# A tiled 90-degree rotation: fewer TensorE outputs in the first macro tile and the last but one, and a different split of the copies

## The chip, the core and the metric

The kernel runs on one core of one Trainium2 chip. The metric is the device time of one execution in microseconds; the median of three runs is given. The engines are TensorE (PE, with its weight loads as PEld), VectorE (DVE), ScalarE (ACT), GpSimd (POOL) and SyncE (SP). Sixteen DMA engines move the data between HBM and the on-chip memory.

## The reference

```python
x = np.random.randn(8192, 8192).astype(np.float32)   # k = 1
return np.rot90(x, k)
```

The output is the input turned by 90 degrees: row i of the output is column 8191 - i of the input. Nothing is computed. 268.4 MB are read, 268.4 MB are written, and on the way each block must be transposed with its columns in reversed order.

## The kernel before, in words

**Tiles.** The input is cut into 16 macro tiles (`kk` 0 to 15) of 1024 rows by 4096 columns. A macro tile has T = 8 loads of 128 rows x 4096 columns (2 MB each; load m belongs to macro tile m // 8 and is called row tile t = m % 8) and J = 8 outputs (n = 8 kk + j; 512 input columns by 1024 rows, 2 MB each).

**Buffers.** Five buffers of 2 MB: buffers 0 and 1 take the landings, 2 to 4 the finished outputs. In the first macro tile loads 0 to 4 use all five, then load 5 goes to buffer 0, 6 to 1, 7 to 2, 8 to 4, 9 to 0, 10 to 1, 11 to 0 and so on by turns. Outputs 0 to 7 use buffers 3, 2, 4, 3, 2, 4, 3, 2. Between them stands `ring`, 63 slots of 128 x 512 elements; a row tile fills eight slots, and the slots that output t of one macro tile leaves free take row tile t of the next.

**Two ways of turning a block.** `by_pe(kk)` lists the outputs that are turned by TensorE. For these DVE copies the landed columns to the ring with the order reversed (`tensor_copy`), TensorE transposes 32 blocks of 128 x 128 into PSUM, and ACT copies PSUM into the output buffer (three copies). For all other outputs ("moved" outputs) DVE transposes within squares of 32 x 32 as it copies to the ring (`transpose`, STREAM_TRANSPOSE in the profile), and 16 copies of 32 x 1024 elements (`moves`) then put the squares in place. `shares(n)` gives the first `BY_DVE` = 3 of these moves to DVE, the next `BY_POOL` = 8 to POOL, and the remaining 5 to ACT. In the last macro tile the split is 6, 6 and 4.

Before the change TensorE turns all eight outputs of macro tile 0, outputs 0 and 4 of macro tiles 1 to 13, outputs 0, 2, 4, 6, 7 of macro tile 14 (the last but one) and 0, 1, 3, 5, 7 of macro tile 15.

**Order on the engines.** Each engine runs its own list in order.

- SP issues loads 1, 3, 5 and half of loads 6 to 9, and then all stores in the order of n. It waits for POOL's last move of a moved output (`s_pool`), or for ACT's last copy of the others.
- ACT issues the other loads. Load n + 9 stands behind output n in ACT's list: `load_behind(n)` puts it in front of the first copy of an output of TensorE, behind all of ACT's moves of a moved output, or behind the third one if the output before was TensorE's. A load waits until the row tile before it in its buffer has been copied out (`taken`).
- POOL makes its share of the moves; its last one waits for the shares of ACT and DVE (`s_act`, `s_dve`).
- DVE takes row tile m = n + 8 after its moves of output n, and only once output n has left the ring: it waits for `s_pool` of a moved output, or for TensorE (`s_half`).
- The 512 columns of the last output in the last row tile of each macro tile have no slot: DVE copies them within the landing buffer, and TensorE turns them there (the "corner") before it turns the last row tile of output 0. In that row tile DVE takes the columns in the order of `got`: output 0's, the moved ones, the corner, the remaining ones of TensorE.

Copies with equal operands in successive pairs of macro tiles run as a loop (`Program.play` with `first` and `times`): ACT and POOL loop over macro tiles 1 to 12, DVE and TensorE over 2 to 13; the others are written out.

```python
        (nc.gpsimd, by_gpsimd, 1, 6),
        (nc.vector, by_vector, 2, 6),
        (nc.tensor, by_tensor, 2, 6),
        (nc.scalar, by_scalar, 1, 6),
```

All recorded instructions stand under line 106 (`Op.run`) in the profile.

Of the kernel before, what the change touches and what calls it, by code (L numbers as in the profile page):

```python
# [13 lines left out]
J = W // (G * P)  # L14
# [6 lines left out]

Q = 32
BY_DVE = 3
BY_POOL = 8
LAST_DVE = 6
LAST_POOL = 6
LAST_PE = [0, 1, 3, 5, 7]
BY_PE = [0, 4]
# [147 lines left out]
def kernel(tc: tile.TileContext, x: bass.AP, k: bass.AP, out: bass.AP):  # L176
    nc = tc.nc
# [6 lines left out]
    KK = len(macros)  # L184
# [11 lines left out]
    outs = [(*o, [(j, g * P) for j in reversed(o[2]) for g in range(G)]) for o in outs]  # L196

    def by_pe(kk):
        if kk == 0:
            return list(range(J))  # L200
        if kk == KK - 1:
            return LAST_PE
        return BY_PE if kk < KK - 2 else [*range(0, J, 2), J - 1]

    def in_quadrants(kk, j):
        return j not in by_pe(kk)
# [127 lines left out]
    for m in range(n_load):  # L334
        kk, t = divmod(m, T)
        here = by_pe(kk)
        rest = [j for j in range(J) if j not in here]
        if kk == KK - 1:
            got = [here, rest] if t < T - 1 else [here[:1], here[1:-1], rest, here[-1:]]
        elif t < T - 1:  # L340
            got = [here, rest]
        else:
            inner = [j for j in here if 0 < j < J - 1]
            got = [here[:1], [j for j in rest if j < J - 1], [J - 1], inner]
        got = [part for js in got for part in split(js)]
        pieces[m] = got
        for js in got:
            done += 1
            for j in js:
                rev[m, j] = done  # L350
# [37 lines left out]
    def shares(n):  # L388
        d, g = (BY_DVE, BY_POOL) if n < n_out - J else (LAST_DVE, LAST_POOL)
        return pairs[:d], pairs[d : d + g], pairs[d + g :]  # L390
# [243 lines left out]
    for e, by, first, times in (  # L634
        (nc.sync, by_sync, None, 0),
        (nc.gpsimd, by_gpsimd, 1, 6),
        (nc.vector, by_vector, 2, 6),
        (nc.tensor, by_tensor, 2, 6),
        (nc.scalar, by_scalar, 1, 6),
    ):  # L640
        program = Program()
        by(program)
        program.play(nc, e, first, times)
# [39 lines left out]
```

## Time and profile before

| | |
|---|---|
| median of 3 runs | 1258.81 us (1258.65 to 1258.83) |
| the profiled execution | 1258.87 us; its span 1257.5 us |
| busy: DVE, POOL, ACT, PE | 783.5, 749.2, 601.7, 293.6 us |
| DMA | 537.05 MB, mean 427 GB/s over the span |
| moves: POOL, ACT, DVE | 666, 417, 261 instructions |
| TensorE transposes | 1460 |

The span runs from the first to the last recorded instruction; the time of the execution has 1.4 us around it. The rows of slices give busy tenths in 40 equal parts of the span, and the row of GB/s gives what the DMA engines moved in each. A group of instructions is read as: line, engine, operation, output <- input, number; then total busy time and the mean of one. In a timeline the first two numbers are the start and the length in microseconds.

### The profile page before, as it was taken

The page shows a single profiled execution, that of the slowest core. Times are in us where ns is not written, and L with a number is a line of the kernel's source. Part 1 is how long each engine was busy: PE and PEld are TensorE (multiplying, and loading weights), DVE is VectorE, ACT ScalarE, POOL GpSimd, SP SyncE. Part 2 cuts the span into 40 slices and gives each one's busy share as a digit, 9 for nine tenths or more (in the row PEclk, how much of TensorE's full clock was granted, in tenths as well). Part 3 has the DMA queues.
Part 4 walks back from the last instruction along what each step waited for, and adds up shares of the span by engine and source line. Part 5 has one row for each costly group of instructions (what it writes and reads, how often), then busy time and mean ns, then how long its engine had stood idle before and what let it go on. Part 6 is the DMA issues. An engine that isn't in the chain of part 4 may idle for free.

```text
span 1257.5 us, 6240 instructions
## 1 busy us (share of the span) xinstructions
PE 293.6 (23%) x1460; PEld 257.4 (20%) x1460; DVE 783.5 (62%) x568; ACT 601.7 (48%) x562; POOL 749.2 (60%) x672
## 2 busy tenths in 40 slices
PE   1566013130131301213022130221302213024261
PEld 0455012120121201212012120221302213023261
DVE  2544866567666676566765667656666566664563
ACT  0334364553655436544365443654436544364374
POOL 0000966668656686666866668666685666864334
PEclk9977556555565655655555555555555555556587
DMA  9999999999999999999999999999999999999999
GB/s 400 416 432 427 430 429 429 429 430 429 431 428 430 430 429 430 429 430 430 430 429 429 429 430 429 430 429 430 429 429 429 429 430 429 430 427 430 428 419 384
DMA packets 36942, 537.05 MB, mean 427 GB/s; under 512 B 4160, under 2 KB 4160, under 8 KB 4160
## 3 DMA queue, kind: packets, MB, share of 16 engines
q1 hardware_dynamic: 19184, 278.93, 52.2%
q10 hardware_dynamic: 17744, 257.96, 48.0%
q8 instruction: 6, 0.10, 0.0%
q14 instruction: 8, 0.07, 0.0%
HBM read 268.44 MB, written 268.44 MB: 427 GB/s over the span
## 4 chain that ended last, share of the span: by engine, by line
DMA 70%; DVE 20%; POOL 3%; issue 3%; PE 1%; ACTq 0%; ACT 0%; DVEq 0%; POOLq 0%; SPq 0%
DMA buf<-in_x_dram 69%; DVE ring L106 18%; POOL buf L106 3%; DVE buf L106 2%; DMA out_dram<-buf 1%; PE ps L106 1%; ACTq L106 0%; ACT buf L106 0%; DVEq L103 0%; DVEq L147 0%; ACTq L103 0%; POOLq L153 0%; POOLq L103 0%; ACTq L430 0%; SPq L422 0%
## 5 line engine op out<-in xcount | busy, mean ns | idle before, releaser
L106 POOL COPY buf<-ring 32x1024 f32<-32x1024 f32 (+1 forms) x666 | 748.5, 1124 | 488.1 <-DMA out_dram<-buf 216.2
L106 ACT COPY buf<-ring 32x1024 f32<-32x1024 f32 (+1 forms) x417 | 427.3, 1025 | 190.1 <-DMA out_dram<-buf 140.0
L106 PE MATMUL ps<-head,ring 128*128 128x128 f32 x1400 | 280.5, 380 | 878.4 <-ACT buf L106 550.1
L106 PEld LDWEIGHTS ps<-head,ring 128*128 128x128 f32 x1400 | 247.2, 202 | 908.9 <-ACT buf L106 560.2
L106 DVE COPY ring<-buf 128x1024 f32<-128x1024 f32 (+4 forms) x159 | 149.0, 947 | 452.6 <-DMA buf<-in_x_dram 415.0
L106 ACT COPY buf<-ps 128x2048 f32<-128x2048 f32 (+4 forms) x143 | 173.2, 1253 | 444.4 <-DMA out_dram<-buf 179.6
L106 DVE STREAM_TRANSPOSE ring<-buf 128x3072 f32<-128x3072 f32 (+1 forms) x133 | 372.1, 2805 | 0.0
L106 DVE COPY buf<-ring 32x1024 f32<-32x1024 f32 (+1 forms) x261 | 274.6, 1052 | 2.5
L106 PE MATMUL ps<-head,buf 128*128 128x128 f32 x60 | 16.1, 422 | 63.1 <-DVE buf L106 63.1
L106 PEld LDWEIGHTS ps<-head,buf 128*128 128x128 f32 x60 | 10.5, 211 | 68.6 <-issue 61.2
L106 DVE COPY buf<-buf 128x512 f32<-128x512 f32 x15 | 5.8, 387 | 0.0
L106 ACT ACT_TABLE_LOAD x1 | 1.3, 1283 | 3.3 <-PEq L430 3.3
L106 POOL MEMSET head<- 128x128 f32 x1 | 0.2, 204 | 2.8 <-POOLq L430 2.8
L106 POOL TENSOR_SCALAR_AFFINE_SELECT head<-head 128x128 f32<-128x128 f32 x1 | 0.3, 292 | 0.2 <-POOL head L106 0.2
L664 POOL MEMSET const-float32-0.0<- 128x1 f32 x1 | 0.1, 97 | 0.2 <-issue 0.2
L106 ACT COPY head<-head 128x1 f32<-128x1 f32 x1 | 0.2, 191 | 0.0
L664 POOL MEMSET const-bfloat16-1.0<- 128x1 bf16 x1 | 0.1, 100 | 0.0
L664 POOL MEMSET const-uint8-127<- 128x1 uint8 x1 | 0.1, 100 | 0.0
L664 POOL MEMSET const-float32-1.0<- 128x1 f32 x1 | 0.1, 98 | 0.0
## 6 DMA issues: line engine op xcount, KB each, us to landing
out_dram<-buf SPq DMA_DIRECT2D x128, 2048.0 KB, 16.7
buf<-in_x_dram ACTq DMA_DIRECT2D x121, 2048.0 KB, 15.2
buf<-in_x_dram SPq DMA_DIRECT2D x3, 2048.0 KB, 17.3
buf<-in_x_dram SPq DMA_DIRECT2D x4, 1024.0 KB, 16.0
buf<-in_x_dram ACTq DMA_DIRECT2D x4, 1024.0 KB, 16.6
```

The source lines that it names most:

```text
L106: i = getattr(e, self.name)(*self.args, **kwargs)
L664: nc = _bacc.Bacc("TRN2", target_bir_lowering=False, num_devices=1)
```

## The change

Three things are changed. TensorE turns only outputs 0 and 4 of macro tile 0, as in the macro tiles after it, and outputs 0, 4, 6, 7 of macro tile 14. For moved outputs outside the last macro tile POOL makes seven moves and ACT six. And TensorE's loop covers macro tiles 1 to 12, so that macro tile 13 is written out and macro tile 1 is in the loop.

```diff
-BY_POOL = 8
+BY_POOL = 7
...
     def by_pe(kk):
-        if kk == 0:
-            return list(range(J))
         if kk == KK - 1:
             return LAST_PE
-        return BY_PE if kk < KK - 2 else [*range(0, J, 2), J - 1]
+        return BY_PE if kk < KK - 2 else [*BY_PE, J - 2, J - 1]
...
-        (nc.tensor, by_tensor, 2, 6),
+        (nc.tensor, by_tensor, 1, 6),
```

With `BY_PE = [0, 4]` seven outputs go from TensorE to moves: 1, 2, 3, 5, 6 and 7 of macro tile 0, and 2 of macro tile 14.

## The prediction

> **What bounds the kernel now.** I read the page first, above all its rows of slices.
>
> ```profile
> DMA  9999999999999999999999999999999999999999
> GB/s 400 416 432 427 430 429 429 429 430 429 431 428 430 430 429 430 429 430 430 430 429 429 429 430 429 430 429 430 429 429 429 429 430 429 430 427 430 428 419 384
> ...
> q8 instruction: 6, 0.10, 0.0%
> ...
> DMA 70%; DVE 20%; POOL 3%; issue 3%; PE 1%; ACTq 0%; ACT 0%; DVEq 0%; POOLq 0%; SPq 0%
> ```
>
> The DMA engines are busy in every slice and move the same 429 or 430 GB/s in all but the first two and the last two. No compute engine is above 62%. So an edit can change the time only where it changes what the DMA engines lose, and they lose little. The trace's packet records say how little: a packet of 16 KB takes 0.611 us, a load or store of 2 MB is 128 packets on 16 engines, so 8 x 0.611 = 4.89 us, and 256 of them are 1251.3 us. The first packet starts at 1.96. 1253.3 is thus the floor of a span of 1257.5.
>
> The windows of the span, in steps of 20 us and then of 2, show where the other 4.2 us are (columns: stretch, length, busy of PE, PEld, DVE, ACT, POOL with counts, clock, DMA share, GB/s).
>
> ```profile
> 40.00:60.00 20.00, 13.19 (x76) 11.67 (x76) 10.53 (x8) 8.28 (x7) 0.00 (x0) 1.00 1.00 410
> ...
> 600.00:620.00 20.00, 0.00 (x0) 0.00 (x0) 14.55 (x10) 9.77 (x10) 17.96 (x16) 0.50 1.00 428
> ...
> 1222.00:1224.00 2.00, 1.73 (x8) 1.73 (x9) 1.98 (x2) 2.00 (x3) 1.84 (x2) 0.51 0.87 369
> 1224.00:1226.00 2.00, 2.00 (x14) 2.00 (x13) 1.97 (x3) 1.98 (x3) 1.96 (x2) 0.64 0.82 344
> ...
> 1254.00:1256.00 2.00, 0.00 (x0) 0.00 (x0) 0.00 (x0) 0.00 (x0) 0.00 (x0) 0.50 0.10 41
> ```
>
> In packets: 0.44 us go to slow packets in the first 5 us and 0.82 between 49 and 53, where loads 0 to 9 end and store 0 begins (packets of 1.1 us, share still 1.00). Store 122 comes late at 1223.6 and costs 15 engines about 0.5. At the end 15 engines stop by 1254.6 and one goes on alone to 1257.1: it is 2.5 us behind. In the middle nothing is lost, though DVE, ACT and POOL work as they will after the change.
>
> Then the timeline of the head, which is what the change rebuilds.
>
> ```profile
> 13.23 4.49 DVE L106 COPY ring<-buf 128x4096 f32<-128x4096 f32 x2 [13.23 <-DMA buf<-in_x_dram]
> ...
> 37.76 2.29 DVE L106 COPY ring<-buf 128x4096 f32<-128x4096 f32 x1 [0.58 <-DMA buf<-in_x_dram]
> ...
> 42.56 0.43 DVE L106 COPY ring<-buf 128x512 f32<-128x512 f32 x1 [2.51 <-DMA buf<-in_x_dram]
> ...
> 43.50 0.71 PEld L106 LDWEIGHTS ps<-head,buf 128*128 128x128 f32 x4 [2.68 <-DVE buf L106]
> ...
> 46.12 74.13 SPq L106 DMA_DIRECT2D out_dram<-buf  x9
> ...
> 63.78 0.69 DVE L106 COPY ring<-buf 128x1024 f32<-128x1024 f32 x1 [6.65 <-DMA buf<-in_x_dram]
> 64.39 3.37 DVE L106 STREAM_TRANSPOSE ring<-buf 128x3072 f32<-128x3072 f32 x1
> ...
> 112.59 0.43 DVE L106 COPY ring<-buf 128x512 f32<-128x512 f32 x1 [5.73 <-DMA buf<-in_x_dram]
> 112.93 2.90 DVE L106 STREAM_TRANSPOSE ring<-buf 128x1536 f32<-128x1536 f32 x2
> 115.75 0.39 DVE L106 COPY buf<-buf 128x512 f32<-128x512 f32 x1
> ...
> 122.55 4.21 ACT L106 COPY buf<-ring 32x1024 f32<-32x1024 f32 x4 [2.87 <-DMA out_dram<-buf]
> ```
>
> DVE now needs 2.3 us for a row tile of macro tile 0 and waits for each landing; a mixed tile, as at 63.78, takes 3.98. Store 0 is issued at 46.12, while the queues still hold loads 8 and 9, and load 10 at 45.5 (ACT's queue). So the DMA never runs dry.
>
> **Part 1: macro tile 0, the DVE.** Row tiles 0 to 6 cost 3.98 instead of 2.3. Loads land in pairs at 13.23, 23.00, 32.68, then at 37.76 and 42.56. Tiles 0 and 1: 13.23 to 21.19. Tiles 2, 3: 23.00 to 30.96. Tiles 4, 5: 32.68 to 36.66 and 40.64. Tile 6 (landed 37.76): 40.64 to 44.62. So far this hides: the landings still come as before, because load 8 is issued at 36.7 and load 9 at 40.6, and the DMA reaches them only at 1.96 + 0.44 + 8 x 4.89 = 41.5 and at 46.4. Loads 0 to 9 end at 51.3.
>
> Tile 7 starts at 44.62 instead of 42.56. Its corner copy now stands behind the moved columns: 115.75 - 112.59 = 3.16 later, 47.78, done at 48.17, TensorE at 48.21. From TensorE's corner to store 0 the trace has 46.12 - 43.50 = 2.62, so store 0 goes out at 50.83, 4.7 us later than now.
>
> **Part 2: load 10.** This is the step that costs. Before, output 1 is TensorE's and load 10 is issued in front of its first copy. After, output 1 is a moved one, and for j = 1 `load_behind` puts the load behind all of ACT's moves, so load 10 stands behind six of them. ACT is free at 50.8; six at 4.21 / 4 = 1.05 are 6.3, so load 10 is issued at 57.2.
>
> What hides that wait is store 0 alone. From issue to first packet on idle engines I take 1.2 us: store 122 is issued at 1223.61 in the timeline and its packets start at 1224.82 (the first load, at the very start, took 1.04). Store 0 runs from 52.0 to 56.9; then the engines wait until 57.2 + 1.2 = 58.4. Store 1 can't help: DVE's three moves stand behind tile 8 (50.2 to 54.2, it waits for TensorE's output 0) and end at 57.4, POOL's last move ends at 58.5.
>
> By 58.4 eleven transfers are done: 58.4 - 1.96 - 11 x 4.89 = 2.7 us lost, where the kernel now has lost 0.44 + 0.82 = 1.26. **Net 1.4 us later.** Whether the slow packets around 50 return does not matter, since they fall into the gap. Slow packets at the restart: none to 0.44, the amount of the start; I take 0.2.
>
> Trainium skill, "DMA: Bandwidth & Descriptors", section "Latency and other measured facts", gives about 0.6 us to the first byte for these queues; by that the net would be 0.8 instead of 1.4 (estimate). The trace has 1.04 and 1.2 and I go by it.
>
> From there the queues fill: load 10 and store 1 give work to 68.2, load 11 is issued behind output 2's moves at 63.7 and store 2 at 67, load 12 at 71. Each is early by 3 us or more. DVE's new wait for POOL's output 1 at tile 9 (to 58.5) delays that tile and load 11 behind it, within this margin.
>
> **Part 3: seven moves for POOL, six for ACT.** Each moved output costs POOL 1.12 less and ACT 1.05 more. Between macro tiles 2 and 13 loads that stand behind all of an output's moves are issued at least 2.0 us after ACT's last move (ACT's rows against its issues), because they wait for DVE; so 1.05 more is hidden, and nothing is lost there anyway (600 to 620). Without that cover it would be 1.05 per load only once both queues were empty. Gain: none, as POOL is not the bound. Zero, with -0.2 to +0.3 for ends.
>
> **Part 4: output 2 of macro tile 14 and TensorE's loop.** The macro tile then has the pattern of tiles 1 to 13, which runs at 429 GB/s, with two TensorE outputs at its end. POOL gets 7 x 1.12 = 7.9 us within an output's 9.8. Zero; the late store 122 may move by its own 0.5 either way, but the engine that ends last is behind by more than that gap and does not see it.
>
> **Part 5: instructions fetched.** TensorE loses 6 x 32 - 4 + 32 = 220 transposes, so 440 instructions with the weight loads. The six 16 KB packets of q8 are TensorE's: between those at 58.2 and 97.2 it runs 256 recorded instructions. 440 are 1.7 packets of 0.6 to 1.0 us less. Each delays one DMA engine, and only the last one counts: 0 to -1.7, I take one packet, -0.6. The instructions that DVE, ACT and POOL gain are fetched in 8 KB packets of 0.31: +0.3 at most, the same doubt.
>
> **Sum.** 1.4 + 0.2 - 0.6 = +1.0 on 1258.87, 1259.9; the median lies 0.06 below its profiled execution, so 1259.8. A measurement can tell about 0.2% from no change, 2.5 us here; this is within.
>
> **The rivals.**
>
> *A, slower: POOL and DVE take turns.* If DVE's copies kept POOL from moving, each moved output would cost POOL 7.9 + 3.2 + 0.7 = 11.8 instead of 7.9, more than the 9.8 that a load and a store need. Outputs 1 to 3 and 5 to 7 would then each be 2 us late, with empty queues in the head: first at store 2, then at 3, some 3 us in all after the queues' reserve. It decides from 9.8 per output. 1259.8 + 3 = 1262.8. For: POOL's moves go from 1.03 to 1.40 beside DVE's. Against: macro tiles 1 to 13 run eight such moves with no loss. 0.12. Trainium skill, "SBUF — State Buffer", section "Who interferes with whom", has such a lock between GpSimd and DVE copies; POOL's mean of 1124 ns over 666 moves does not bear out a full block.
>
> *B, no difference: the fetches pay for the gap.* 1.4 - 1.7 = -0.3 and quick restart: 1258.5. For: the last engine's lag has steps of 0.6 at 58 and at 616, after instruction packets. Against: the packet at 97 hit another engine. 0.25.
>
> *C, the lagging engine catches up.* It works on while others wait, so gaps shrink its 2.5 us. If all of it goes: 1258.8 + 1.6 - 2.5 = 1257.9, and with all of part 5 besides 1256.2. Its lag is still under 1 us in the head, so the new gaps come too early. 0.08, of which a quarter for the lower value.
>
> **How the numbers follow.** Forecast 0.55 (1259 to 1261.2), A 0.12, B 0.25, C 0.08. Slower by over 0.2%, above 1261.3: most of A and a little of the forecast, if load 10 is 1.5 us later than summed, 0.13. Faster: 0.02. Range: B's and C's upper part to the lower edge of A, 1257.9 to 1261.8.
>
> **What would show it.** Right: GB/s of 40 to 60 at about 380 instead of 410 (20 us less 2.2 to 2.5, at 429); store 0 issued near 50.8, load 10 near 57.2; no loss from 70 to 1220; 1240 transposes on PE; POOL 634 moves, some 713 us, ACT 540 moves; fewer q8 packets. Wrong: a second dip between 60 and 90 (A), load 10 before 56, or all engines ending together (C).

## The result, and the profile after

The changed kernel takes 1260.37 us (median of 20 runs, 1260.01 to 1260.84) against 1258.78 us (20 runs, 1258.57 to 1259.09): 1.6 us more, a ratio of 1.0013, 95% interval 1.0007 to 1.0018. It is a small loss that these runs can tell from none, and within the 0.2% that the prediction counted as no change.

The page of the changed kernel, rows of slices, the queue of TensorE's instructions and the chain:

```profile
DMA  9999999999999999999999999999999999999999
GB/s 399 402 432 427 430 430 429 431 427 431 429 431 429 429 431 428 431 429 431 429 429 431 428 431 429 431 429 429 431 428 431 429 430 430 429 431 427 432 417 385
...
q8 instruction: 4, 0.07, 0.0%
...
DMA 71%; DVE 20%; issue 4%; POOL 2%; ACT 1%; PE 0%; ACTq 0%; DVEq 0%; POOLq 0%; SPq 0%
```

The middle is what it was. The second slice falls from 416 to 402, and the last two hardly move. POOL has 634 moves and 694 us, ACT 540 moves and 702 us, TensorE 1240 transposes: the work went where the diff sends it.

Windows of the changed kernel (stretch, length, busy of PE, PEld, DVE, ACT, POOL, clock, DMA share, GB/s):

```profile
40.00:60.00 20.00, 6.45 (x27) 5.35 (x27) 16.91 (x14) 13.35 (x13) 9.34 (x9) 0.92 0.99 406
600.00:620.00 20.00, 0.00 (x0) 0.00 (x0) 13.53 (x11) 11.88 (x12) 15.19 (x14) 0.50 1.00 428
...
50.00:52.00 2.00, 1.65 (x8) 1.65 (x9) 2.00 (x2) 1.96 (x3) 1.92 (x3) 1.00 0.83 352
54.00:57.00 3.00, 0.00 (x0) 0.00 (x0) 2.97 (x3) 2.95 (x4) 2.07 (x2) 0.99 1.07 344
60.00:63.00 3.00, 0.00 (x0) 0.00 (x0) 3.00 (x2) 2.94 (x3) 2.92 (x3) 0.50 0.96 300
```

Three places lose. Around 51 the share falls to 0.83: the engines are idle for 0.34 us. At 54 to 57 and at 60 to 63 the share is about 1.00, yet little is moved: the packets are slow. In the packet records each of the 16 engines has a packet of 1.20 us instead of 0.61 at 55.4 to 55.8, right before load 10's first packet at 56.6, and packets of up to 1.25 us before store 1's first at 62.9. The kernel before has one such slow spell, at 49 to 53; the changed kernel has two and the idle stretch. Counted against 0.611 us per packet, the DMA engines lose 1.9 us between 40 and 120, where the kernel before lost 0.8. The 15 engines that end together do so at 1255.8 instead of 1254.65, the same 1.1 later; the last one trails them by 2.2 us instead of 2.45, so the span grows by 0.84 in these two executions. The profiled execution took 1260.05, that is 1.66 around its span of 1258.39, where it was 1.32 before.

The head of the changed kernel, from its timeline:

```profile
44.15 0.38 DVE L106 COPY ring<-buf 128x512 f32<-128x512 f32 x1
44.45 2.89 DVE L106 STREAM_TRANSPOSE ring<-buf 128x1536 f32<-128x1536 f32 x2
47.27 0.38 DVE L106 COPY buf<-buf 128x512 f32<-128x512 f32 x1
...
47.70 0.72 PEld L106 LDWEIGHTS ps<-head,buf 128*128 128x128 f32 x4 [6.00 <-DVE buf L106]
...
50.33 2.10 ACT L106 COPY buf<-ring 32x1024 f32<-32x1024 f32 x2
50.33 71.98 SPq L106 DMA_DIRECT2D out_dram<-buf  x9
...
51.39 0.34 ACTq L106 DMA_DIRECT2D buf<-in_x_dram  x1
52.43 10.53 ACT L106 COPY buf<-ring 32x1024 f32<-32x1024 f32 x10
...
58.62 1.54 DVE L106 COPY ring<-buf 128x1024 f32<-128x1024 f32 x1 [1.26 <-POOL buf L106]
```

The corner copy (47.27) does come behind the moved columns, and store 0 is issued at 50.33. But load 10, ACTq at 51.39, stands between ACT's first and second move of output 1, though in ACT's list it is behind all six. The sixth ends only at 56.6. So ACT's sequencer, which issues the DMAs, had gone past five moves that had not ended.

### The profile page after: what moved, and what is told of

The parts are those of the page before. It is cut to its first block, busy times and chain, and to the rows that moved or that the text cites. A ratio compares the mean times of both kernels' runs of the same rounds, so it can differ in the third digit from the quotient of the medians.

```text
span 1258.4 us, 5902 instructions
## 1 busy us (share of the span) xinstructions
PE 263.9 (21%) x1240; PEld 230.2 (18%) x1240; DVE 781.5 (62%) x606; ACT 702.3 (56%) x664; POOL 694.0 (55%) x640
## 4 chain that ended last, share of the span: by engine, by line
DMA 71%; DVE 20%; issue 4%; POOL 2%; ACT 1%; PE 0%; ACTq 0%; DVEq 0%; POOLq 0%; SPq 0%
DMA buf<-in_x_dram 71%; DVE ring L106 19%; POOL buf L106 2%; DVE buf L106 2%; ACT buf L106 1%; PE ps L106 0%; ACTq L106 0%; DVEq L103 0%; POOLq L103 0%; DVEq L147 0%; ACTq L428 0%; ACTq L103 0%; SPq L420 0%
## 5 line engine op out<-in xcount | busy, mean ns | idle before, releaser
L106 POOL COPY buf<-ring 32x1024 f32<-32x1024 f32 (+1 forms) x634 | 693.3, 1093 | 544.1 <-ACT buf L106 175.7
L106 ACT COPY buf<-ring 32x1024 f32<-32x1024 f32 x540 | 553.3, 1025 | 135.1 <-DVE ring L106 81.2
L106 PE MATMUL ps<-head,ring 128*128 128x128 f32 x1180 | 250.3, 395 | 890.0 <-ACT buf L106 531.4
L106 DVE COPY ring<-buf 128x1024 f32<-128x1024 f32 (+2 forms) x159 | 147.7, 937 | 455.2 <-DMA buf<-in_x_dram 440.1
L106 DVE STREAM_TRANSPOSE ring<-buf 128x3072 f32<-128x3072 f32 (+2 forms) x150 | 403.0, 2698 | 0.0
L106 PEld LDWEIGHTS ps<-head,ring 128*128 128x128 f32 x1180 | 219.7, 210 | 917.5 <-ACT buf L106 536.1
L106 ACT COPY buf<-ps 128x512 f32<-128x512 f32 (+4 forms) x122 | 147.8, 1247 | 399.6 <-DMA out_dram<-buf 182.2
L106 DVE COPY buf<-ring 32x1024 f32<-32x1024 f32 (+1 forms) x282 | 244.4, 867 | 2.7
```

The lines of the kernel that those rows point to most:

```text
L106: i = getattr(e, self.name)(*self.args, **kwargs)
```

## The experiments

All are compared with runs of the kernel before, whose medians were 1258.84, 1258.87 and 1258.99 us beside them.

**The head alone.** The kernel before with one edit:

```diff
         if kk == 0:
-            return list(range(J))
+            return BY_PE
```

> The kernel before with one part of the change: outputs 0 and 4 alone by TensorE in macro tile 0; POOL keeps eight moves, macro tile 14 and TensorE's loop are as before. Theory H (the loss of 1.6 us sits in the head: store 0 and load 10 go out late, the DMA queues run low between 50 and 64 us): 1260.4, within 0.3. Rival S (the seven-to-six split, macro tile 14 or the loop cost it): within 0.3 of 1258.8.

1261.13 us (1259.67 to 1262.03), ratio 1.0018 (1.0009 to 1.0027). Rival S falls. The head carries the loss, and more than all of it: 0.8 more than the whole change and above H's 1260.4. Between 80 and 100 this kernel loses 1.2 us, which the changed kernel does not; the last experiment comes back to that. The profiled execution is the fastest of the eleven. From 40 to 120 its DMA engines lose 3.0 us, but its last engine ends only 0.1 us behind the next one (2.45 in the kernel before), so that most of the loss does not show in its time. That is what rival C described, but in this one execution.

**The rest alone.**

```diff
-BY_POOL = 8
+BY_POOL = 7
...
-        return BY_PE if kk < KK - 2 else [*range(0, J, 2), J - 1]
+        return BY_PE if kk < KK - 2 else [*BY_PE, J - 2, J - 1]
```

> The kernel before with the other parts: seven moves for POOL and six for ACT, outputs 0, 4, 6, 7 of macro tile 14 by TensorE; macro tile 0 stays wholly with TensorE, and its loop with macro tiles 2 to 13. Theory H: 1258.8, within 0.3. Rival S: 1260 or more, and a loss in the packets of the middle or the end.

1258.88 us, ratio 1.0000 (0.9991 to 1.0009). With macro tile 0 left to TensorE, the split and macro tile 14 cost nothing. Its profiled execution loses 1.1 us between 40 and 120, with the head of the kernel before, which lost 0.8: single executions differ by some 0.3.

**Load 10 in front.** The changed kernel with

```diff
     def load_behind(n):
         kk, _, js, _ = outs[n]
+        if n == 1:
+            return 0
```

> The changed kernel with load 10 issued in front of ACT's moves of output 1 instead of behind them. In the changed kernel load 10 left at 51.4, when ACT had ended one of six moves, and not at 57.2. Theory Q (ACT's sequencer runs ahead of its moves, so that the place of load 10 behind them costs some 1.5 us and not 6): load 10 at about 49.8, right behind load 9 in its queue, no idle DMA at 51 and one spell of slow packets less: 1259.3 to 1259.9. The prediction's step (six moves must end first): 1.2 to 1.4 us faster than the changed kernel, 1259.0.

1260.15 us, ratio 1.0010 (1.0001 to 1.0019): 0.2 less than the changed kernel, and neither expectation holds. Load 10 is issued at 49.73 as expected and the place behind the moves turns out to matter little, which speaks for Q's reading of the sequencer. But the time was not won: store 0, issued 0.6 later, now had to start behind load 10, 0.23 of the idle 0.34 at 51 stayed, and the slow packets lasted from 51 to 56. The DMA lost 1.9 us in 40 to 60:

```profile
40.00:60.00 20.00, 6.55 (x27) 5.35 (x27) 16.90 (x14) 13.34 (x13) 9.33 (x9) 1.00 0.99 388
```

**Load 10 behind the moves in fact.** The changed kernel with

```diff
+            if n == 1:
+                e.wait_ge(s_act, 1)
             if due == len(steps):
                 load_behind_output(e, n)
```

> The changed kernel with a wait for ACT's six moves of output 1 in front of load 10, so that it is issued when the sixth has ended, near 56.8. This is the step as the prediction summed it. Theory Q: the DMA stands idle from the end of store 0, near 57, to 58.0, some 1.0 to 1.4 us more lost than in the changed kernel: 1261.3 to 1261.8. The prediction's step (the changed kernel already waits for them): the same time as the changed kernel, 1260.4.

1262.09 us (1261.68 to 1262.49), ratio 1.0025 (1.0016 to 1.0035): 1.7 more than the changed kernel and 0.3 above Q's range. Two lines of this kernel's timeline:

```profile
50.31 6.31 ACT L106 COPY buf<-ring 32x1024 f32<-32x1024 f32 x6
...
56.65 0.34 ACTq L106 DMA_DIRECT2D buf<-in_x_dram  x1
```

and two of its windows:

```profile
56.00:58.00 2.00, 0.00 (x0) 0.00 (x0) 1.33 (x2) 1.59 (x2) 0.62 (x2) 1.00 0.50 107
58.00:60.00 2.00, 0.00 (x0) 0.00 (x0) 1.39 (x1) 1.98 (x3) 1.90 (x3) 1.00 0.75 295
```

This is the head as the prediction had drawn it: load 10 at 56.65 (predicted 57.2), its first packet at 57.62, and idle engines before (share 0.50, 107 GB/s), 1.3 us of it where the prediction had 1.5. But the step costs more than it summed. Against the kernel before this run takes 3.25 us more (0.34 of it outside the span), where the prediction had 1.4 and 0.2: after the idle stretch load 10's packets are slow too (up to 1.6 us; 0.6 lost by 60), and 1.2 more are lost after 60, most of it before store 1 starts at 63.5. The step was right in kind, and the changed kernel does not take it.

**The corner first.** The changed kernel with the corner of macro tile 0 in front of the moved columns:

```diff
             got = [here[:1], [j for j in rest if j < J - 1], [J - 1], inner]
+            if kk == 0:
+                got = [here[:1], [J - 1], [j for j in rest if j < J - 1], inner]
```

> The changed kernel with the corner of macro tile 0 copied right behind output 0's columns of row tile 7, in front of the moved columns. Store 0 should be issued near 47.6 instead of 50.3, before load 9 has ended at 51, and load 10 near 49.2, so that both stand queued and start together as in the kernel before. Theory H2 (the loss in the head comes from store 0 and load 10 reaching the DMA late and one at a time: an idle 0.34 us and a second spell of slow packets of 0.75 us): some 1.0 us faster than the changed kernel, 1259.1 to 1259.6. Rival M (the moved outputs of macro tile 0 as such cost it, by the pace of POOL and DVE): the same as the changed kernel, 1260.2 or more.

1259.22 us (1258.74 to 1260.04), ratio 1.0003 (0.9994 to 1.0012): 1.15 less than the changed kernel, and no longer told from the kernel before. H2's forecast holds and M falls, since the moved outputs are still there.

```profile
44.53 0.43 DVE L106 COPY buf<-buf 128x512 f32<-128x512 f32 x1
44.87 2.90 DVE L106 STREAM_TRANSPOSE ring<-buf 128x1536 f32<-128x1536 f32 x2
...
47.63 0.63 SPq L106 DMA_DIRECT2D out_dram<-buf  x1
...
49.18 0.34 ACTq L106 DMA_DIRECT2D buf<-in_x_dram  x1
```

In its timeline store 0 goes out at 47.63 and load 10 at 49.18, while load 9 is still on the engines. Its packets have no idle stretch and one slow spell instead of two; 0.8 us is lost between 40 and 120, as before the change, and 40 to 60 moves 412 GB/s instead of 406:

```profile
40.00:60.00 20.00, 6.43 (x27) 5.35 (x27) 18.67 (x15) 15.54 (x15) 10.83 (x10) 0.85 1.00 412
```

The run takes away the idle stretch and the slow spell at once and does not say what each costs by itself. The 0.35 that is left to the kernel before is time outside the span (1.62 to 1.74 us, against 1.26 to 1.39).

**Both first.** The corner first and load 10 in front of output 1's moves.

```diff
+            if kk == 0:
+                got = [here[:1], [J - 1], [j for j in rest if j < J - 1], inner]
...
+        if n == 1:
+            return 0
```

> Both edits: the corner first, and load 10 in front of ACT's moves of output 1. Theory H2: as the run with the corner first alone or up to 0.3 faster, 1258.9 to 1259.6, since load 10 stood in its queue in time already. Rival M: 1260.2 or more.

1259.14 us, ratio 1.0003 (0.9994 to 1.0012): as with the corner alone.

**TensorE's loop.**

```diff
-        (nc.tensor, by_tensor, 1, 6),
+        (nc.tensor, by_tensor, 2, 6),
```

> The changed kernel with TensorE's loop over macro tiles 2 to 13 as before, macro tile 1 written out. The time outside the span was 1.65 to 1.7 us in three kernels with the loop from macro tile 1 and 1.27 to 1.37 in three with the loop from 2. Theory L (the loop's place sets that): the span unchanged, 0.3 us less outside it, 1260.0 to 1260.2. Rival (it is scatter): 1260.4.

1260.46 us, ratio 1.0013 (1.0004 to 1.0022), and 1.66 around the span. Theory L falls: the loop's place costs nothing and does not set the time outside the span.

**The corner first and the loop from 2.**

```diff
+            if kk == 0:
+                got = [here[:1], [J - 1], [j for j in rest if j < J - 1], inner]
...
-        (nc.tensor, by_tensor, 1, 6),
+        (nc.tensor, by_tensor, 2, 6),
```

> The corner first together with TensorE's loop over macro tiles 2 to 13. Theories H2 and L together: the loss of the change is gone, 1258.7 to 1259.2, no different from the kernel before. Rival M: 1259.9 or more.

1259.15 us, ratio 1.0001 (0.9992 to 1.0011): as the corner alone; the loop adds nothing here either.

**Eight moves for POOL in the changed kernel.**

```diff
-BY_POOL = 7
+BY_POOL = 8
```

> The changed kernel with eight moves for POOL and five for ACT, as before the change; macro tile 0, macro tile 14 and the loop as changed. In the first run with the head alone and eight moves, outputs 1 to 3 of macro tile 0 left POOL 10.35 us apart, above the 9.8 of a load and a store, and 1.2 us more were lost between 80 and 100; with seven moves they were 9.6 apart and nothing was lost there. Theory P8 (in the head, where no finished outputs are in reserve, the pace of POOL and DVE counts and the seventh move matters): 10.3 apart again, 1260.9 to 1261.4. Rival (the split is hidden everywhere): 1260.4. The profiled time outside the span, 1.66 in the changed kernel against 1.3 with eight moves or with macro tile 0 as before, is read as well: 1.3 if the split makes it.

1262.00 us (1260.24 to 1262.65), ratio 1.0022 (1.0012 to 1.0032): 3.0 more than the kernel before beside it, where the changed kernel has 1.6 more, so 1.4 to 1.6 slower than with seven, and more than P8 gave. POOL and DVE in the timeline, first with eight moves:

```profile
58.37 9.67 POOL L106 COPY buf<-ring 32x1024 f32<-32x1024 f32 x8 [0.68 <-DVE buf L106]
...
68.72 9.67 POOL L106 COPY buf<-ring 32x1024 f32<-32x1024 f32 x8 [0.68 <-DVE buf L106]
...
79.06 8.94 POOL L106 COPY buf<-ring 32x1024 f32<-32x1024 f32 x8 [0.68 <-DVE buf L106]
80.20 1.54 DVE L106 COPY ring<-buf 128x1024 f32<-128x1024 f32 x1 [1.27 <-POOL buf L106]
```

then with seven, the changed kernel:

```profile
57.49 8.23 POOL L106 COPY buf<-ring 32x1024 f32<-32x1024 f32 x7 [1.38 <-DVE buf L106]
...
67.09 8.23 POOL L106 COPY buf<-ring 32x1024 f32<-32x1024 f32 x7 [1.38 <-DVE buf L106]
```

The window from 80 to 100 with eight moves:

```profile
80.00:100.00 20.00, 4.57 (x19) 3.78 (x19) 13.65 (x9) 13.79 (x13) 12.40 (x13) 0.59 0.99 394
```

and with seven:

```profile
80.00:100.00 20.00, 4.58 (x19) 3.78 (x19) 12.25 (x9) 16.20 (x15) 13.35 (x13) 0.50 1.01 432
```

POOL and DVE wait for each other by turns: POOL's groups begin 10.35 us apart with eight moves and 9.60 apart with seven, and a load and a store need 9.78. At 10.35 the reserve of queued transfers shrinks: load 11 has its first packet 3.3 us after its issue (64.36 to 67.62), load 13 only 2.1 (85.06 to 87.14; with seven moves 3.6). From there to 100 the DMA engines lose 1.5 us, and the window moves 394 GB/s instead of 432. The share is still 0.99: the engines are idle for less than 0.1 us, and what is lost is lost in slow packets of up to 1.64 us. That the eighth move costs this is shown; why the packets turn slow when the reserve is small is not. The time outside the span is 1.68 here, so the split does not make it either.

## Why the prediction was right, and what in it was not

The forecast of a small loss within 0.2% held: 1259.8 against 1260.37, +1.0 against +1.6. The argument that carried it is that only the head, where no finished outputs stand in reserve, can lose DMA time; the runs with the head alone and with the rest alone bear that out. Rivals B (1258.5) and C (1257.9) fall with the measured loss. That the size came so near is in part luck. The prediction had 1.4 for an idle gap, 0.2 for slow packets and -0.6 for instruction packets; the changed kernel has 0.34 of idle time, 0.75 of slow packets and 0.34 outside the span. Of the signs that it named, two went against it: load 10 was issued before 56, and 40 to 60 moved 406 GB/s and not 380. The dip at 60 to 63, which it gave to rival A, has another cause, since it goes with the corner first while POOL and DVE work as before.

- *Part 1, the DVE in macro tile 0:* right. Store 0 was to be issued at 50.83 and was at 50.33; a row tile took 3.86 to 3.94 instead of 3.98.
- *Part 2, load 10:* the step that failed. It was taken to be issued at 57.2, when the sixth move has ended. It was issued at 51.39, when the first had: ACT's sequencer had gone past the other five. The trace of before has a small sign of this, which the prediction did not use: a load is issued at 147.09, before the five moves that began at 142.07 end, at 147.33:

```profile
142.07 5.26 ACT L106 COPY buf<-ring 32x1024 f32<-32x1024 f32 x5 [4.52 <-DMA out_dram<-buf]
...
147.09 0.34 ACTq L106 DMA_DIRECT2D buf<-in_x_dram  x1
```

So the idle gap of 1.5 us before 58.4 is not there. The run that makes load 10 wait has 1.3 us of it, and takes 1.7 us more. Part 2 also set a delay of 0.6 us against 1.04 and 1.2 from issue to first packet. In that run the 0.97 us from 56.65 to 57.62 contain 0.34 us of the issue itself; from its end it is 0.63, so these values may be one delay counted from two points.

- *In its place:* 0.34 idle at 51, because store 0 is late, and a second spell of slow packets, 0.75 us. The prediction said that the slow packets did not matter since they would fall into the gap. The second spell is the larger part of the loss. The run with the corner first removes both, and with them 1.15 us.
- *Part 3, the split:* zero for macro tiles 1 to 13, right. In the head the term is not zero: with eight moves the change would have cost 3.0 us instead of 1.6. Rival A had the threshold of 9.8 per output right, but its 11.8 took POOL and DVE to shut each other out; the pace is 10.35 with eight moves, 9.60 with seven, just on the good side. The Trainium skill, "SBUF — State Buffer", section "Who interferes with whom", describes a full block between GpSimd and a DVE copy in a two-port mode. Here DVE's and POOL's copies overlap, at 1.4 us for a move of either instead of 1.03 on POOL and 0.68 on DVE; that is less than the 1.71 of one after the other.
- *Part 4, macro tile 14 and the loop:* zero, as the run of the rest alone and that of the loop show.
- *Part 5, instructions:* six 16 KB packets became four, as 1.7 fewer foretold. That this shortens the time is not shown. The last engine's lag fell by 0.3, not 0.6, in the two profiled executions, but in the other kernels with four such packets it is anywhere from 0.1 to 2.6 us, and in the rest alone, with six, 1.4.
- *Missed:* 0.34 us outside the span. It is there in all twenty executions of the changed kernel (1.60 to 1.71 us, where the runs of the kernel before have 1.26 to 1.39; spans are on record to 0.1) and in every kernel that has both macro tile 0 and macro tile 14 changed (1.65 to 1.69 in eight profiled executions). The rest alone does not have it (1.28 to 1.36); the head alone has 1.27 to 1.33 in seven of eleven executions and 1.51 to 2.36 in four. What makes it stays open.

The sum by what was measured: 1.1 lost in the head, 0.3 won at the last engine, 0.34 outside the span: 1.2 between the two profiled executions (1260.05 and 1258.87). The remaining 0.4 is the place of these two among their runs: the profiled execution of the changed kernel is 0.32 below its median. Over all executions the median span is 1258.7 against 1257.5, that is the 1.1 of the head within 0.1, and 0.3 more lie outside it.

No version was found that beats the kernel before. The corner first gives its time back with fewer TensorE outputs, no more.

## What to carry to other kernels

In a kernel like this one, whose DMA engines never rest, look for the stretches where no work is in reserve, here the first 15 us after the last plain load (50 us with eight moves on POOL), and follow there what puts each transfer into its queue; the rest was hidden here. A DMA that stands behind copies in an engine's list need not be held until they end: see in the trace how far the issue runs ahead before counting that wait, and see which small piece of work (here one corner copy of 0.4 us behind 2.9 us of others) holds the first store. A share of work that is free in the steady state can decide the start: there the pace of the chain counts against the pace of the DMA.

## What the runs showed of the hardware that was not expected

A transfer that met one of the other direction (here also of the other queue) alone on the engines started late. Load 10, issued at 51.39 beside store 0, had its first packet at 56.6 (5.2 us); store 1, issued at 58.55 beside load 10, at 62.9 (4.4 us); load 11, issued at 63.48 beside store 1, at 67.2 (3.7 us). On idle engines it was 1.0 us (issue at 56.65, packet at 57.62). At the first two of these meetings the lone transfer's last packets also took about twice 0.61 us, and each of these spells cost 0.75 to 0.8 us. At the third under 0.1 us was lost, and in the run with eight moves 0.05 us in all between 62 and 82, where loads and stores also follow each other alone. So meeting a lone transfer is not enough to make packets slow. Between 130 and 1200, where loads and stores stand queued together, 6 of the changed kernel's 28052 packets took over 0.8 us; among the loads alone, from 5 to 48, none did. What makes a spell slow was not tested.

ACT issued a DMA while five of its copies were still to end: with six moves in front, load 10 went out when the first ended (51.39); with five, when the first began, in the run with eight moves for POOL:

```profile
50.46 1.04 ACT L106 COPY buf<-ring 32x1024 f32<-32x1024 f32 x1
...
50.47 0.34 ACTq L106 DMA_DIRECT2D buf<-in_x_dram  x1
```
